# A decoder layer's sparse attention: the compressed keys are set in front of the selected keys, so that one product gives both scores for six of eight query tiles

## The chip, the cores and the metric

The kernel runs on one core of one Trainium2 chip. The metric is device time in microseconds (us) for one execution of the whole program. The profile is of one such execution; its engines are PE (matrix products), DVE (vector), ACT (activation functions), POOL (a second, slower vector engine) and SP (which issues transfers).

## What is computed

One decoder layer on 1024 tokens of width 1024: a sparse attention ("NSA", eight query heads in two key groups) and a latent attention ("MLA", eight heads) side by side, merged by gates, then a gated feed-forward part with a short convolution, then a gated input embedding. The change is in NSA. Each query there attends three times, and the three results are gated and added:

```python
# compressed: 63 keys per group, each made from 32 tokens (stride 16)
s_c = einsum('btgrd,bjgd->bgrtj', q, k_cmp) * scale - slopes * dist_c
p_cmp = masked_softmax(s_c, dist_c >= 0)          # dist_c = t - end of block j
o_cmp = einsum('bgrtj,bjgd->btgrd', p_cmp, v_cmp)
# selected: the 16 best blocks of 64 keys; with 1024 tokens there are 16, so all of them
s = einsum('bcgrd,bgckld->bgrckl', qc, kg) * scale - slopes * dist
pr = masked_softmax(s, dist >= 0)
o_sel = einsum(..., pr, vg)
# window: the last 512 keys
o_win = einsum('bgrqs,bsgd->bqgrd', masked_softmax(...), vblk)
o = g[:, :, 0] * o_cmp + g[:, :, 1] * o_sel + g[:, :, 2] * o_win
```

The softmax of each of the three is its own: own maximum, own sum.

## The kernel before

**Tiles and units.** The 1024 queries are eight tiles of 128, numbered i. NSA goes through them from 7 to 0. For a tile and a key group g (0, 1) there are three units, called by b: b=1 selected, b=2 window, b=0 compressed, in this order. A unit has four heads r of 64 dimensions. A unit's score steps give its probabilities (tokens in partitions, keys along a row); its second part, once per 128 keys, transposes the four heads' block on PE (L885, into a tile `pT`, three buffers), splits it into a rounded high part on ACT (`ph`, L308) and the rest on DVE (`pl`, L309), and multiplies both with the values into `oT` (L894 and L895).

**Keys and queries.** A score is a sum of two 128-row products. `KA` holds the high part of the keys twice, `KB` the low part with two rows for position; `QA` and `QB` are the queries that go with them, `QB` with the slopes. For the compressed keys there are `KAc` and `KBc`, 64 columns wide (63 keys and a zero column). Masks are added by a product of an identity (`identb`, bfloat16) with a table of zeros and -1e30: `mdiag` for the diagonal block, `mfar` for the window's far end, `mcmp` for compressed keys not yet complete.

**Selected and window scores.** For tiles 4 to 7 `s_step` does one head at a time: `KB` product (L941), masks (L944, L945), `KA` product (L948), into a score tile `sc` of two PSUM banks. `sc` has two buffers in all. DVE takes the row's maximum (L869), ACT the exponential straight from PSUM with the sum on the side (L873), DVE the reciprocal (L875), POOL multiplies by sum and gate (L954). Rows of up to 512 keys stand in one bank, longer ones are two halves. For tiles 0 to 3 `s_group` does four heads (tiles 0, 1) or two (tiles 2, 3) in one `sc` tile (L979, L981, L983; maximum L985, exponential L987). A product is never less than 256 columns wide there.

**Compressed scores.** `c_step` is a score step of its own. Per head it has three products of 64 columns (L915, L916, L917). Then, on all four heads in one instruction each: maximum (L920), its clamp (L921) and the subtraction into `PC` in SBUF (L922) on DVE, the exponential on ACT (L924), the sum (L925), its clamp, reciprocal and gate (L926 to L928) on DVE, the product on POOL (L929). `PC` is one buffer for all tiles.

**Order.** `attend` gives every score step and every block step a time in steps of a list and sorts by it; unit k's score steps lie between `lo` and `last`, and each unit's `lo` is no earlier than the `last` of the unit before it. A scheduler that simulates the engines then settles the order of instructions on each engine. PE, DVE and ACT run their instructions in order. The branch products of an earlier part (L303 to L305) are strewn in as fills in the later tiles.

## Time and profile before

| what | us |
|---|---|
| runs | 1784.37, 1789.68, 1800.34; median 1789.68 |
| the profiled execution | 1789.02, its span 1787.2 |
| first NSA product to the end of tile 4's scores | 407 to 580 of the span |
| tiles 3 to 0 of NSA | 580 to about 692 |
| busy over the span: PE, weight load, DVE, ACT, POOL | 1713.3, 1403.3, 1272.1, 860.8, 292.1 |

A busy time says how long an engine had an instruction in it. PE's instructions overlap: the time from the start of one to the start of the next is what one of them takes of PE; its own duration is longer. Where an engine idles, the row says which engine's instruction ended the wait.

### The profile page before, as it was taken

To read this page: it belongs to the slowest core of one execution; us is meant where nothing else is said; L and a number is where in the kernel's file an instruction comes from. 1 tells how busy PE (TensorE), PEld (TensorE's weight loads), DVE (VectorE), ACT (ScalarE), POOL (GpSimd) and SP (SyncE) were. 2 spreads that over 40 slices of the span, in tenths; PEclk is the share of its full clock that TensorE was granted. 3 is DMA by queue.
4 is the path that set the end of the run, shared out by engine and by line. 5 is a ranking of instruction groups with operands and counts; after the bars stand their busy time and mean duration, and the time that the engine had idled before them with its cause. 6 is when DMAs were issued, how large, how long until landed. Compare 5 with 4: busy or idle time off the path is not lost.

```text
span 1787.2 us, 23559 instructions
## 1 busy us (share of the span) xinstructions
PE 1713.3 (96%) x8537; PEld 1403.3 (79%) x8537; DVE 1272.1 (71%) x2030; ACT 860.8 (48%) x1537; POOL 292.1 (16%) x435
## 2 busy tenths in 40 slices
PE   8969899999999999999899999999999998999998
PEld 7857688887777787887678887888888876887886
DVE  6557754425888887787765698888888879767553
ACT  6433332325777766666543354444444443345321
POOL 3000004003555544333401000000000000001010
PEclk8989899999999999999999999999999999999999
DMA  5295242200001225656383112222223292438111
GB/s 194 80 243 154 71 134 69 59 25 30 1 1 37 89 70 158 149 151 183 110 261 109 57 55 83 83 83 94 71 83 94 71 348 87 147 122 274 58 59 47
DMA packets 182512, 191.94 MB, mean 107 GB/s; under 512 B 12805, under 2 KB 136125, under 8 KB 182397
## 3 DMA queue, kind: packets, MB, share of 16 engines
q1 hardware_dynamic: 175292, 180.91, 33.2%
q10 hardware_dynamic: 7104, 9.54, 1.5%
q8 instruction: 67, 1.10, 0.2%
q14 instruction: 49, 0.39, 0.1%
HBM read 142.96 MB, written 47.45 MB: 107 GB/s over the span
## 4 chain that ended last, share of the span: by engine, by line
PE 80%; DVE 8%; DMA 7%; ACT 2%; issue 2%; SPq 1%; POOL 1%; DVEq 0%; POOLq 0%; ACTq 0%
PE big L304 9%; PE big L303 9%; PE big L305 9%; PE pT L303 6%; PE pT L304 6%; PE pT L305 6%; PE pT L885 5%; PE one L303 3%; PE one L304 3%; PE one L305 3%; PE oT L895 3%; PE oT L894 3%; DMA k_d<-kx 1%; DVE wlo L309 1%; PE sc L948 1%
## 5 line engine op out<-in xcount | busy, mean ns | idle before, releaser
L345 POOL TENSOR_SCALAR stat<-stat 128x1 f32<-128x1 f32 (+1 forms) x48 | 18.2, 380 | 892.5 <-ACT yn L1278 624.9
L309 DVE TENSOR_TENSOR pl<-pT,ph 128x512 fp32r<-128x512 f32 (+1 forms) x244 | 149.6, 630 | 13.7 <-ACT ph L308 12.2
L308 ACT ACTIVATE ph<-pT 128x512 fp32r<-128x512 f32 (+1 forms) x244 | 130.1, 555 | 60.7 <-PE pT L885 52.9
L303 PE MATMUL big<-hh,rh 128*128 128x512 f32 x380 | 148.2, 390 | 2.5 <-ACT e L220 1.0
L304 PE MATMUL big<-hl,rh 128*128 128x512 f32 x380 | 148.0, 389 | 0.0
L305 PE MATMUL big<-hh,rl 128*128 128x512 f32 x380 | 147.5, 389 | 0.0
L869 DVE TENSOR_REDUCE mx<-sc 128x1 f32<-128x640 f32 (+7 forms) x128 | 106.6, 835 | 32.4 <-PE sc L948 22.6
L308 ACT ACTIVATE rh<-S 128x512 fp32r<-128x512 f32 x100 | 62.8, 629 | 115.3 <-PE big L304 78.0
L1401 DVE SCALAR_TENSOR_TENSOR u<-C,wcT,u 128x1024 f32<-128x1024 f32 x88 | 111.0, 1280 | 3.7 <-ACT u L1397 3.2
L308 ACT ACTIVATE rh<-wraw 128x512 fp32r<-128x512 f32 x83 | 51.9, 630 | 114.2 <-PE big L304 47.1
L304 PE MATMUL big<-wlo,whi 128*128 128x512 f32 x242 | 97.0, 401 | 9.9 <-DVE wlo L309 9.9
L305 PE MATMUL big<-whi,wlo 128*128 128x512 f32 x242 | 95.2, 393 | 0.0
L303 PE MATMUL pT<-hh,whi 128*128 128x512 f32 x224 | 89.8, 401 | 5.1 <-DVE kx L309 3.3
L303 PE MATMUL big<-whi 128*128 128x512 f32 x242 | 91.3, 393 | 2.4 <-ACT whi L308 2.4
L304 PE MATMUL pT<-hl,whi 128*128 128x512 f32 x224 | 89.0, 397 | 0.0
L305 PE MATMUL pT<-hh,wlo 128*128 128x512 f32 x224 | 88.9, 398 | 0.0
L303 PEld LDWEIGHTS big<-hh,rh 128*128 128x128 f32 x380 | 71.2, 188 | 18.6 <-ACT e L220 1.5
L309 DVE TENSOR_TENSOR rl<-S,rh 128x512 fp32r<-128x512 f32 x100 | 68.7, 689 | 22.0 <-ACT rh L308 21.9
L304 PEld LDWEIGHTS big<-hl,rh 128*128 128x128 f32 x380 | 71.4, 188 | 15.0 <-DVE hl L309 0.4
L305 PEld LDWEIGHTS big<-hh,rl 128*128 128x128 f32 x380 | 71.4, 188 | 14.8
L308 ACT ACTIVATE whi<-wraw 128x1024 fp32r<-128x1024 f32 x40 | 42.1, 1058 | 53.0 <-DVE wraw L1463 20.9
L304 PEld LDWEIGHTS big<-wlo,whi 128*128 128x128 f32 x242 | 45.9, 190 | 24.7 <-DVE wlo L309 15.4
(543 smaller groups left out, 5003.2 us busy)
## 6 DMA issues: line engine op xcount, KB each, us to landing
wraw<-in_w_up_dram SPq DMA_DIRECT2D x44, 512.0 KB, 3.9
wraw<-in_w_in_dram SPq DMA_DIRECT2D x24, 512.0 KB, 4.7
g<-gm_d SPq DMA_DIRECT2D x48, 256.0 KB, 3.4
wraw<-in_w_down_dram SPq DMA_DIRECT2D x47, 256.0 KB, 3.3
g_d<-u SPq DMA_DIRECT2D x22, 512.0 KB, 2.6
wraw<-g_d SPq DMA_DIRECT2D x36, 256.0 KB, 3.0
xt<-in_x_dram SPq DMA_DIRECT2D x16, 512.0 KB, 6.8
gm_d<-gms ACTq DMA_DIRECT2D x16, 512.0 KB, 2.9
```

What stands on the lines that cost most here:

```text
L303: nc.tensor.matmul(ps, lh, rh, start=start, stop=False, skip_group_check=more)
L304: nc.tensor.matmul(ps, lh, rl, start=False, stop=False, skip_group_check=more)
L305: nc.tensor.matmul(ps, ll, rh, start=False, stop=stop, skip_group_check=more)
L308: nc.scalar.activation(hi, ps, AF.Copy)
L309: nc.vector.tensor_sub(lo, ps, f32(hi))
L345: nc.gpsimd.tensor_scalar(st, st, EPS, None, op0=OP.add)
L869: nc.vector.tensor_reduce(u.nm[:, r:r + 1], src, axis=AX.XY, op=OP.max, negate=True)
L885: nc.tensor.transpose(pT[:m, r], cols(r), ident)
L894: nc.tensor.matmul(oT[:, a:], v, ph, start=first, stop=False)
L895: nc.tensor.matmul(oT[:, a:], v, pl, start=False, stop=last)
L948: nc.tensor.matmul(ps[:, si, :w], q_part(0, 128, i, 4 * g + r), KA[b - 1][g][:, k0 + o:k0 + o + w], start=False, stop=True)
L1401: nc.vector.scalar_tensor_tensor(u[s], C[s][:, 2 - sh:2 - sh + T], wcT[:, 2 - sh, ch:ch + 1], u[s], op0=OP.mult, op1=OP.add)
```

## The change

The compressed keys and the selected keys of a group now stand in one tile, `CKA` and `CKB`, 64 + 1024 columns: `KAc`, `KBc` are its first 64 columns, `KA[0]`, `KB[0]` the rest. For the selected unit of tiles 0, 1, 2, 4, 5, 6 the first 64 columns are scored in the same product as the selected keys (`c0` = 64), the mask `mcmp` is added there, and `c_heads` does the compressed softmax from the score tile: maximum (L924 of the new file) per head or group on DVE, one exponential of 64 columns per head straight from PSUM with its sum (L929), reciprocal and gate (L934, L935), POOL's product into a new tile `pcm` of two buffers. Tiles 3 and 7, whose rows of 512 and 1024 keys leave no room in the banks, keep `c_step`. The selected unit of tile 1 is done in two groups of two heads. The compressed unit has no score step for the six tiles, and a unit without score steps no longer moves `last`.

```diff
--- before.py
+++ after.py
@@ -256,7 +256,8 @@
         lo = max(lo, last, start[k] - 24.0)
         if u.after is not None:
             lo = max(lo, start[k - 1] + u.after)
-        last = max(start[k] - 8.0, lo + 1.0)
+        if u.S:
+            last = max(start[k] - 8.0, lo + 1.0)
         if u.hook is not None:
             ev.append((start[k] + u.at, -1, u.hook))
         for j, f in enumerate(u.S):
@@ -704,10 +705,10 @@
     Vc = [vp0([128, 128], F32R, f"Vc{g}") for g in range(2)]
     V0 = vp0([128, 4, 4, 128], F32R, "V0")
     kv = Pool("kv", side="left")
-    KA = [[kv([128, T], F32R, f"KA{b}{g}") for g in range(2)] for b in range(2)]
-    KB = [[kv([128, T], F32R, f"KB{b}{g}") for g in range(2)] for b in range(2)]
-    KAc = [kv([128, 64], F32R, f"KAc{g}") for g in range(2)]
-    KBc = [kv([128, 64], F32R, f"KBc{g}") for g in range(2)]
+
+    CK = [[kv([128, 64 + T], F32R, f"C{n}{g}") for g in range(2)] for n in ("KA", "KB")]
+    KA, KB = ([[c[:, 64:] for c in CK[n]], [kv([128, T], F32R, f"K{'AB'[n]}1{g}") for g in range(2)]] for n in range(2))
+    KAc, KBc = ([c[:, :64] for c in CK[n]] for n in range(2))
 
     sm = Pool("sm", side="right")
     gls = [sm([64, 126], F32, f"gl{n}") for n in range(2)]
@@ -909,6 +910,31 @@
         segs = segments(n)
         pc = PC
 
+        both = b < 2 and i not in (3, 7)
+        c0 = 64 if both and b else 0
+
+        def c_heads(r0, n_r, src):
+
+            if r0 == 0:
+                c = st["pc", i, g] = Unit()
+                stats_of(c)
+                c.P = bq([128, 4, 64], F32, "pcm", bufs=2)
+            c = st["pc", i, g]
+            nm = c.nm[:, r0:r0 + n_r]
+            nc.vector.tensor_reduce(nm, src, axis=AX.X, op=OP.max, negate=True)
+            if i == 0:
+                nc.vector.tensor_scalar(nm, nm, 1e20, None, op0=OP.min)
+            for j in range(n_r):
+                r = r0 + j
+                nc.scalar.activation(c.P[:, r], src[:, j], AF.Exp, bias=c.nm[:, r:r + 1], accum_out=c.sums[:, r:r + 1])
+            if r0 + n_r == 4:
+                sums = c.sums
+                if i == 0:
+                    nc.vector.tensor_scalar(sums, sums, 1e-30, None, op0=OP.max)
+                nc.vector.reciprocal(sums, sums)
+                nc.vector.tensor_mul(sums, sums, gates[:, i, g * 4:g * 4 + 4])
+                nc.gpsimd.tensor_tensor(c.P, c.P, sums[:, :, None].to_broadcast([128, 4, 64]), op=OP.mult)
+
         def c_step():
             ps = two_banks()[:, 0, :256].rearrange("p (b m) -> p b m", m=64)
             for r in range(4):
@@ -937,17 +963,27 @@
                     u.P = [P[:, j] for j in range(4)]
                     stats_of(u)
                 ps = two_banks()
+
+                def keys(si, o, w, K):
+                    if c0 and si == 0:
+                        return ps[:, 0, :64 + w], K[0][g][:, :64 + w]
+                    return ps[:, si, c0:c0 + w], K[1][b - 1][g][:, k0 + o:k0 + o + w]
+
                 for si, (o, w) in enumerate(segs):
-                    nc.tensor.matmul(ps[:, si, :w], qb[:, r], KB[b - 1][g][:, k0 + o:k0 + o + w],
-                                     start=True, stop=False)
+                    out_, k_ = keys(si, o, w, (CK[1], KB))
+                    nc.tensor.matmul(out_, qb[:, r], k_, start=True, stop=False)
+                if c0:
+                    nc.tensor.matmul(ps[:, 0, :64], identb, mcmp[:, i], start=False, stop=False)
                 if b == 2:
                     nc.tensor.matmul(ps[:, 0, :128], identb, mfar, start=False, stop=False)
-                nc.tensor.matmul(ps[:, len(segs) - 1, segs[-1][1] - 128:segs[-1][1]], identb, mdiag,
-                                 start=False, stop=False)
+                e = c0 + segs[-1][1]
+                nc.tensor.matmul(ps[:, len(segs) - 1, e - 128:e], identb, mdiag, start=False, stop=False)
                 for si, (o, w) in enumerate(segs):
-                    nc.tensor.matmul(ps[:, si, :w], q_part(0, 128, i, 4 * g + r), KA[b - 1][g][:, k0 + o:k0 + o + w],
-                                     start=False, stop=True)
-                src = row_max(u, r, ps, n)
+                    out_, k_ = keys(si, o, w, (CK[0], KA))
+                    nc.tensor.matmul(out_, q_part(0, 128, i, 4 * g + r), k_, start=False, stop=True)
+                if c0:
+                    c_heads(r, 1, ps[:, 0:1, :64])
+                src = row_max(u, r, ps[:, :, c0:], n)
                 pv = u.P[r][:, :n]
                 row_exp(u, r, pv, src)
                 c = b * 8 + g * 4 + r
@@ -972,19 +1008,24 @@
                         u.P[r] = PL["pS"]([128, 512], F32, "pS", bufs=6)
                 w = 1024 // n_r
                 ps = two_banks().rearrange("p a (b m) -> p (a b) m", m=w)
-                w = max(n, 256)
+                w = max(c0 + n, 256)
+                ka, kb = ((CK[a][g] if c0 else K[b - 1][g])[:, :w] for a, K in enumerate((KA, KB)))
                 for j in range(n_r // 2):
                     pair = (j, j + n_r // 2)
                     for r in pair:
-                        nc.tensor.matmul(ps[:, r, :w], qb[:, r0 + r], KB[b - 1][g][:, :w], start=True, stop=False)
+                        nc.tensor.matmul(ps[:, r, :w], qb[:, r0 + r], kb, start=True, stop=False)
                     for r in pair:
-                        nc.tensor.matmul(ps[:, r, n - 128:n], identb, mdiag, start=False, stop=False)
+                        if c0:
+                            nc.tensor.matmul(ps[:, r, :64], identb, mcmp[:, i], start=False, stop=False)
+                        nc.tensor.matmul(ps[:, r, c0 + n - 128:c0 + n], identb, mdiag, start=False, stop=False)
                     for r in pair:
-                        nc.tensor.matmul(ps[:, r, :w], q_part(0, 128, i, 4 * g + r0 + r), KA[b - 1][g][:, :w],
-                                         start=False, stop=True)
-                nc.vector.tensor_reduce(u.nm[:, r0:r0 + n_r], ps[:, :, :n], axis=AX.X, op=OP.max, negate=True)
+                        nc.tensor.matmul(ps[:, r, :w], q_part(0, 128, i, 4 * g + r0 + r), ka, start=False, stop=True)
+                if c0:
+                    c_heads(r0, n_r, ps[:, :, :64])
+                keys = ps[:, :, c0:c0 + n]
+                nc.vector.tensor_reduce(u.nm[:, r0:r0 + n_r], keys, axis=AX.X, op=OP.max, negate=True)
                 for r in rs:
-                    nc.scalar.activation(u.P[r][:, :n], ps[:, r - r0, :n], AF.Exp, bias=u.nm[:, r:r + 1],
+                    nc.scalar.activation(u.P[r][:, :n], keys[:, r - r0], AF.Exp, bias=u.nm[:, r:r + 1],
                                          accum_out=u.sums[:, r:r + 1])
                 nc.vector.reciprocal(u.sums[:, r0:r0 + n_r], u.sums[:, r0:r0 + n_r])
                 c = b * 8 + g * 4
@@ -995,17 +1036,18 @@
             return run
 
         if b == 0:
-            u.S = [c_step]
+            u.S = [] if both else [c_step]
         elif i >= 4:
             u.S = [s_step(r) for r in range(4)]
         else:
-            n_r = 2 if i > 1 else 4
+            n_r = 2 if i > 1 or i == 1 and b == 1 else 4
             u.S = [s_group(r, n_r) for r in range(0, 4, n_r)]
         if b == 1:
             u.S.insert(0, lambda: q_form(i, g))
 
         def t_front(j):
-            return lambda: front(u, j, lambda r: u.P[r][:, j * 128:(j + 1) * 128] if b else u.P[r], 0, 128 if b else 64)
+            return lambda: front(u, j, lambda r: u.P[r][:, j * 128:(j + 1) * 128] if b else
+                                 st["pc", i, g].P[:, r] if both else u.P[r], 0, 128 if b else 64)
 
         def t_back(j):
             def run():
```

The first place is PE between the scores of tile 6 group 0 and group 1. Before (`QB_3215` is group 0's query tile, `QB_3216` group 1's; `hh` and `hl` are buffers of probabilities):

```order
L894 MATMUL oT<-ph,V_2317 128x512
L885 MATMUL pT<-ident,hh_3846 128x128 x4
L915 MATMUL sc<-KBc_2331,QB_3215 128x64
L916 LDWEIGHTS identb
L916 MATMUL sc<-mcmp,identb 128x64
L917 MATMUL sc<-KAc_2329,QA_2712 128x64
...
L885 MATMUL pT<-ident,hh_3846 128x128 x4
L941 MATMUL sc<-KB_2326,QB_3216 128x448 x2
L945 LDWEIGHTS identb
L945 MATMUL sc<-mdiag,identb 128x128
L948 MATMUL sc<-KA_2322,QA_2712 128x448 x2
```

After, the same place (lines of the new file; L886 is the transposition, L895 and L896 the products with the values):

```order
L895 MATMUL oT<-ph,V_2317 128x512
L886 MATMUL pT<-ident,hh_3842 128x128 x4
L974 MATMUL sc<-CKB_2324,QB_3212 128x512
L974 MATMUL sc<-CKB_2324,QB_3212 128x448
L976 LDWEIGHTS identb
L976 MATMUL sc<-mcmp,identb 128x64
L980 LDWEIGHTS identb
L980 MATMUL sc<-mdiag,identb 128x128
L983 MATMUL sc<-CKA_2322,QA_2708 128x512
L983 MATMUL sc<-CKA_2322,QA_2708 128x448
```

The twelve products of `c_step` (four of the three shown) are gone from between the two units; each selected head has its first half 64 columns wider and one mask product more.

The second place is ACT in the same stretch, from the last window heads of group 0 to the second selected head of group 1. Before:

```order
L873 ACTIVATE hl_3977,sums<-sc,mx 128x640 x2
L308 ACTIVATE ph<-pT 128x512 x2
L924 ACTIVATE PC<-PC 128x256
L308 ACTIVATE ph<-pT 128x512 x2
L873 ACTIVATE hl_4112,sums<-sc,mx 128x896
L308 ACTIVATE ph<-pT 128x512
L873 ACTIVATE hl_4112,sums<-sc,mx 128x896
```

After:

```order
L874 ACTIVATE hl_3991,sums<-sc,mx 128x640 x2
L309 ACTIVATE ph<-pT 128x512
L929 ACTIVATE pcm,sums<-sc,mx 128x64
L309 ACTIVATE ph<-pT 128x512
L874 ACTIVATE hl_4069,sums<-sc,mx 128x896
L309 ACTIVATE ph<-pT 128x512
L929 ACTIVATE pcm,sums<-sc,mx 128x64
L309 ACTIVATE ph<-pT 128x512 x2
L874 ACTIVATE hl_4069,sums<-sc,mx 128x896
```

One exponential of 256 columns a unit has become one of 64 columns ahead of each head's own, with copies `ph` queued behind it.

The third place is DVE in that stretch. Before:

```order
L920 TENSOR_REDUCE mx<-sc 128x4
L309 TENSOR_TENSOR pl<-pT,ph 128x512
L921 TENSOR_SCALAR mx<-mx 128x4
L922 TENSOR_TENSOR PC<-sc,mx 128x256
L309 TENSOR_TENSOR pl<-pT,ph 128x512
L869 TENSOR_REDUCE mx<-sc 128x1
L925 TENSOR_REDUCE sums<-PC 128x4
L309 TENSOR_TENSOR pl<-pT,ph 128x512
L926 TENSOR_SCALAR sums<-sums 128x4
```

After:

```order
L924 TENSOR_REDUCE mx<-sc 128x1
L310 TENSOR_TENSOR pl<-pT,ph 128x512
L870 TENSOR_REDUCE mx<-sc 128x1
L310 TENSOR_TENSOR pl<-pT,ph 128x512
L924 TENSOR_REDUCE mx<-sc 128x1
L876 RECIPROCAL sums<-sums 128x1
L310 TENSOR_TENSOR pl<-pT,ph 128x512
L870 TENSOR_REDUCE mx<-sc 128x1
```

Of `c_step`'s seven instructions the clamps, the subtraction and the sum are gone; its maximum is now one small instruction ahead of each head's own.

## Rows read from the trace of the kernel before

**Rows 1.** The windows view of two stretches of the span: NSA tiles 7 to 4, and NSA tiles 3 to 0. Columns: stretch, its length, busy us (and instructions) of PE, of its weight load, of DVE, ACT and POOL, granted clock of PE as a share, busy share of the DMA engines, GB/s.

```profile
407.00:580.00 173.00, 169.49 (x1082) 135.86 (x1080) 137.49 (x286) 120.70 (x248) 81.35 (x92) 1.00 0.06 16
580.00:692.00 112.00, 110.92 (x702) 88.53 (x701) 91.55 (x195) 78.30 (x218) 58.90 (x90) 1.00 0.30 85
```

**Rows 2.** The waits view of PE in 407 to 692, all its rows: the waiting instruction, whom it waited for, us in total, times, the longest.

```profile
PE oT L894 <- DVE osum L1032: 1.3, 2, 0.7
PE oT L895 <- DVE pl L309: 1.2, 5, 0.3
PE sc L941 <- ACT hl L873: 0.6, 3, 0.3
PE sc L915 <- ACT hl L873: 0.5, 1, 0.5
PE sc L979 <- ACT pS L987: 0.4, 1, 0.4
PE oT L894 <- ACT ph L308: 0.3, 1, 0.3
PE sc L979 <- ACT hl L987: 0.2, 1, 0.2
```

**Rows 3.** The timeline of PE over tile 7 group 1's compressed scores: start, duration, line, tiles, shape, count. The rows left out are the second and third head and most of the fourth, which read alike; the last row is the next instruction.

```profile
478.33 0.30 PE L915 MATMUL sc<-KBc,QB 128*128 128x64 f32 x1
478.47 0.20 PE L916 MATMUL sc<-mcmp,identb 128*128 128x64 bf16 x1
478.51 0.28 PE L917 MATMUL sc<-KAc,QA 128*128 128x64 f32 x1
...
479.32 0.28 PE L917 MATMUL sc<-KAc,QA 128*128 128x64 f32 x1
479.44 0.47 PE L895 MATMUL oT<-pl,V 128*128 128x512 f32 x1
```

**Rows 4.** The timeline of PE at places where products of other widths follow each other: a window head's masks, and MLA's scores of 320 and 512 columns.

```profile
474.79 0.23 PE L944 MATMUL sc<-mfar,identb 128*128 128x128 bf16 x1
474.86 0.22 PE L945 MATMUL sc<-mdiag,identb 128*128 128x128 bf16 x1
...
704.07 0.40 PE L1090 MATMUL sc<-hh 96*128 96x512 f32 x1
704.31 0.39 PE L1091 MATMUL sc<-hh 96*128 96x512 f32 x1
...
708.60 0.31 PE L1091 MATMUL sc<-hl 96*128 96x320 f32 x1
708.75 0.31 PE L1095 MATMUL sc<-hl 96*128 96x320 f32 x1
```

**Rows 5.** The view of instruction groups by shape, DVE, 407 to 880: line, tiles, shapes, count, busy us in all, mean ns of one, idle before.

```profile
L985 DVE TENSOR_REDUCE mx<-sc 128x4 f32<-128x1024 f32 x4 | 4.9, 1222 | 1.2 <-PE sc L983 1.2
L985 DVE TENSOR_REDUCE mx<-sc 128x4 f32<-128x512 f32 x4 | 2.8, 688 | 0.8 <-PE sc L983 0.7
L920 DVE TENSOR_REDUCE mx<-sc 128x4 f32<-128x256 f32 x16 | 6.7, 421 | 3.6 <-PE sc L917 3.2
L922 DVE TENSOR_TENSOR PC<-sc,mx 128x256 f32<-128x256 f32 x16 | 6.7, 421 | 1.4 <-PE pT L885 0.3
L925 DVE TENSOR_REDUCE sums<-PC 128x4 f32<-128x256 f32 x16 | 6.5, 408 | 0.2
L921 DVE TENSOR_SCALAR mx<-mx 128x4 f32<-128x4 f32 x16 | 4.3, 267 | 0.2
L926 DVE TENSOR_SCALAR sums<-sums 128x4 f32<-128x4 f32 x16 | 2.8, 174 | 0.0
L927 DVE RECIPROCAL sums<-sums 128x4 f32<-128x4 f32 x16 | 2.7, 169 | 0.1
L928 DVE TENSOR_TENSOR sums<-sums,gates 128x4 f32<-128x4 f32 x16 | 2.6, 161 | 0.2
L869 DVE TENSOR_REDUCE mx<-sc 128x1 f32<-128x128 f32 x8 | 2.3, 286 | 1.4 <-PE sc L1095 1.3
```

**Rows 6.** The same view, ACT: `c_step`'s exponential, the two narrowest exponentials from PSUM, and the instruction that fetches a sum.

```profile
L924 ACT ACTIVATE PC<-PC 128x256 f32<-128x256 f32 x16 | 6.6, 414 | 1.3 <-DVE PC L922 0.5
L987 ACT ACTIVATE pS<-sc,mx 128x256 f32<-128x256 f32 x8 | 3.7, 476 | 0.0
L987 ACT ACTIVATE pS<-sc,mx 128x128 f32<-128x128 f32 x8 | 2.9, 367 | 0.2 <-PE pT L885 0.2
L987 ACT ACTIVATION_READ_ACCUMULATOR pS<-sc,mx 128x1 f32 x32 | 6.7, 209 | 0.0
```

**Rows 7.** The timeline of ACT where two exponentials with sums follow each other in tile 3, with only the fetch of the first one's sum between them.

```profile
601.08 0.69 ACT L987 ACTIVATE pS<-sc,mx 128x512 f32<-128x512 f32 x1
...
601.74 0.70 ACT L987 ACTIVATE pS<-sc,mx 128x512 f32<-128x512 f32 x1
```

**Rows 8.** The waits view of ACT in 407 to 692, its largest row.

```profile
ACT ph L308 <- PE pT L885: 38.8, 52, 2.0
```

**Rows 9.** The timeline of PE and of ACT at the first and the third selected head of tile 6 group 0: the starts of their first products, and the first head's exponential.

```profile
480.34 0.65 PE L941 MATMUL sc<-KB,QB 128*128 128x448 f32 x2
...
483.68 1.00 ACT L873 ACTIVATE hl<-sc,mx 128x896 f32<-128x896 f32 x1
...
485.83 0.65 PE L941 MATMUL sc<-KB,QB 128*128 128x448 f32 x2
```

## The prediction, made blind

> **What bounds the kernel now.** I read the windows of the NSA stage first, then what PE waited for there, then single starts on PE. In the two stretches PE is busy 169.5 of 173 and 110.9 of 112 us, DVE 137.5 and 91.6 (79% and 82%), ACT 120.7 and 78.3 (70% both), at the full granted clock (2.4 GHz) [rows 1]. Busy alone doesn't make PE the bound, since one of its products lies over the next. But the waits of PE in these 285 us come to 1.3 + 1.2 + 0.6 + 0.5 + 0.4 + 0.3 + 0.2 = 4.5 us [rows 2], and starts follow each other as closely as the columns let them: 0.24 us for a 512-column product, 0.15 for a 320-column one [rows 4]. The largest wait of ACT is for transpositions from PE, 38.8 us [rows 8]: ACT is held up by PE and not the other way. So in this stage the price of a product is the time to the next start, and work taken from PE should come off the end nearly whole; work on DVE and ACT has cover as long as PE's few waits don't grow. After the stage comes MLA, which begins on PE where NSA ends, so what is won here is moved forward and not lost in a gap.
>
> **PE, removed.** Four heads of compressed scores take from 478.33 to 479.44, 1.11 us [rows 3]. By head that is 0.14 for the KB product, 0.04 for the mask, and some 0.1 for the KA product: a product of 64 columns costs most of what 256 would. Of 16 units 12 lose this: 12 x 1.11 = 13.3 us.
>
> **PE, added.** Going from 320 to 512 columns lengthens a start by 0.24 - 0.15 = 0.09 [rows 4], so 64 more columns cost 0.03; two products a head, 40 heads of tiles 1, 2, 4, 5, 6: 2.4 us. Tile 0 pays none, since its 128 + 64 columns still fit the 256 that were run anyway. The mask is now one more product in each of 48 heads: 0.04 beside its neighbours in c_step [rows 3], 0.07 for the 128 columns of the far mask [rows 4]. I take 0.04, the same instruction: 1.9 us (3.4 at the other end). The mask stands where another mask product already stood, so no further change between number formats comes with it. Added 4.3. **Net on PE: 13.3 - 4.3 = 9.0 us less.**
>
> **DVE.** c_step's seven instructions are 0.421 + 0.267 + 0.421 + 0.408 + 0.174 + 0.169 + 0.161 = 2.02 us a unit [rows 5]. A maximum over 64 columns has no row; 128 columns are 0.286, 256 are 0.421, so by the same slope 64 are 0.22, and no less than the 0.16 of an instruction on four numbers. Tiles 4 to 6 (six units) now pay 4 x 0.22 + 0.169 + 0.161 = 1.21. Tiles 1 and 2 (four units) pay two maxima over 2 x 64, 2 x 0.286 + 0.33 = 0.90. Tile 0 (two units) keeps its clamps: 0.42 + 0.27 + 0.17 + 0.33 = 1.19. Tile 1's split makes two maxima of 0.69 from one of 1.22, with one reciprocal more (0.17): 0.3 for each of two units, 0.6. Saved: 6 x 0.81 + 4 x 1.12 + 2 x 0.83 - 0.6 = 10.4 us. DVE isn't the bound, so I enter none of it; it pays for the next part.
>
> **ACT.** c_step's one exponential was 0.41. In its place stand four of 64 columns with sums. No row has that width; 0.476 at 256 and 0.367 at 128 give 0.11 per 128 columns, so some 0.31 at 64, and one with its fetch of the sum takes about its own duration to the next start (0.66 for one of 0.69) [rows 6, 7]. So 4 x 0.31 = 1.24, and 0.83 more a unit: 12 x 0.83 = 10 us on ACT in all. If the fetch (0.21) came on top each time it would be 10 + 48 x 0.21 = 20 us. ACT has 86 us of the 285 free [rows 1], and 38.8 of them stand ahead of the copies `ph`, waiting for PE. Entered at nothing: PE's lead over ACT hides it. If that cover fails, the copies `ph` that queue behind each small exponential come late, and PE's products with the values after them.
>
> **POOL, transfers, order.** POOL's product over 4 x 64 columns is the same as before. No transfer is added; two branch loads change places with their neighbours in SP's queue. Each selected head holds its score buffer longer by the small maximum, 0.22, since the head's own maximum queues behind it on DVE; the small exponential runs on ACT while that maximum runs. On the other side twelve score tiles fewer are taken from the same two buffers. At tile 6 the first head's products start at 480.34, its exponential ends at 483.68 + 1.00, and the head that takes the same buffer starts at 485.83 [rows 9]: 1.15 us are free, five times what the small maximum adds. Nothing entered.
>
> **Sum.** The profiled execution took 1789.0 (span 1787.2), 0.7 under the median of the runs. 1789.0 - 9.0 = 1780.0. By the ends of the terms above (mask 0.07, or all of PE's 4.5 us of waits falling away with DVE's saved work) this runs from 1775.5 to 1781.5; with 10 us of ACT half uncovered, to 1785.
>
> A rule speaks against it. PE's weight load is busy 135.9 of 173 us, 79%, while PE's products show 98% [rows 1]. The Trainium skill (Trainium Kernel Development and Optimization, Performance Expectations) holds that the busy time of matrix products is a bad measure of how near a kernel is to its limit, because they are pipelined, and that the share of weight loading is a better one. By that a fifth of PE is slack, and taking work from it need give nothing; the sum would be 0 in place of -9.0. The waits and the starts don't bear it out, so it is a rival with a small chance.
>
> **Rivals.**
> 1. PE isn't the bound (the rule above): the round from transposition over `ph` and `pl` to the products sets the pace, PE's freed time turns into waits, and the time stays at 1789, between 1786 and 1792. For it: PE's busy time overstates; ACT and DVE are both over 70%. Against: 4.5 us of waits in 285. Chance 0.06.
> 2. ACT's queue eats the gain: 48 small exponentials stand ahead of copies `ph`, and their 10 us reach PE in full (half: 1785): 1780 + 10 = 1790. For it: ACT is in order, and PE already waits at times for exponentials (0.6 + 0.5 + 0.4 + 0.2) [rows 2]. Against: ACT's 38.8 us of waiting for PE [rows 8]. Chance 0.12.
> 3. The freed DVE time helps as well: PE's waits for `pl`, `osum` and for buffers shrink, and unit after unit runs with one change of product kind less. The waits are worth 4.5 and all of DVE's 10.4 would be the far end: 1780 - 4.5 to 1780 - 10.4, so 1770 to 1775. For it: the longest waits are for DVE [rows 2]. Against: they are short. Chance 0.11.
> 4. Slower: the score buffers. If each of the 48 heads is released later by small maximum, small exponential and fetch, 0.22 + 0.31 + 0.21 = 0.74, and PE stands for all of it, that is 48 x 0.74 = 35.5, less the 9.0 won: 1815. It decides from the point where a buffer is held longer than PE takes to come round to it again; at tile 6 the room is 1.15 us, so it needs heads that stand closer than those, as in tile 1's two groups and wherever window heads follow. Chance 0.05.
>
> **How the numbers follow.** The likeliest, 1775.5 to 1785, has 0.66. The range takes rival 1, rival 2 and most of the third with it: 1771 to 1792, which leaves out rival 4 and the tails. One per cent of the median is 17.9 us, about what a measurement of this kernel can tell from no change (the three runs lie 16 us apart). Faster by that means below 1771.8: the far end of rival 3, and scatter, 0.09. Slower means above 1807.6: rival 4, 0.05. Between: 0.86. The predicted time is 1780.
>
> **What would show it.** Right: the compressed products fall from 64 to 16 of each kind; NSA's stretch, 285 us before, is shorter by 8 to 10 and what follows has its old length; the 64-column exponentials last 0.3 us; DVE works about 10 us less and ACT about 10 more; PE's waits stay near 4.5 us. Wrong: PE's waits for `ph` or for score buffers rise by several us (rivals 2, 4), or its starts draw apart with no wait named (rival 1). The sum would fail most easily at the 1.11 us, if its neighbours already filled part of it, or at ACT's cover in tiles 2 to 0, where groups of heads send several exponentials at once.

## The result, and the profile after

The changed kernel is 0.6% slower: 1800.99 us in the median against 1789.43 of the kernel before, ratio 1.0061, 95% interval 1.0047 to 1.0075. That is 11 us the wrong way, where 9 the right way were forecast; the time lies outside the range given, 1771 to 1792. "Between" the one-per-cent bounds, given 0.86, came true, but by luck: it was meant for a gain of 9 us, and none came. The profiled execution took 1803.94 us (before 1789.02). Its page, busy time of each engine:

```profile
span 1800.8 us, 23446 instructions
PE 1714.7 (95%) x8441; PEld 1396.5 (78%) x8441; DVE 1265.0 (70%) x2012; ACT 872.5 (48%) x1621; POOL 294.4 (16%) x435
```

DVE does 7.1 us less than before and ACT 11.7 more, nearly what was said. PE has 96 instructions fewer, yet is busy no shorter. The waits view of PE in NSA, and then over the 16 us in which NSA gives way to MLA (line, tile, whom it waited for, us in total, times, the longest):

```profile
PE sc L974 <- ACT hl L874: 3.5, 9, 0.7
PE oT L896 <- DVE pl L310: 1.4, 4, 0.6
PE sc L974 <- ACT hh L874: 1.1, 1, 1.1
PE oT L895 <- DVE osum L1074: 1.0, 3, 0.7
...
PE sc L1132 <- ACT pS L1028: 3.2, 2, 2.7
```

Before, all waits together were 4.5 us and those for score buffers the smaller part [rows 2]. Now the largest are PE's waits to write scores (`sc`) until an exponential (L874, L1028) has read the buffer. Behind the 2.7 us one something else shows. The windows view of that place (length, then busy us of PE, weight load, DVE, ACT, POOL, and the granted clock):

```profile
680.00:684.00 4.00, 4.00 (x34) 3.43 (x32) 2.75 (x6) 2.53 (x11) 2.61 (x5) 1.00 0.44 133
684.00:688.00 4.00, 1.86 (x10) 0.96 (x9) 3.69 (x10) 3.34 (x12) 0.61 (x1) 1.00 0.46 132
688.00:692.00 4.00, 3.47 (x12) 2.04 (x13) 0.89 (x3) 1.65 (x10) 2.43 (x5) 0.71 1.04 222
692.00:696.00 4.00, 3.47 (x14) 2.59 (x13) 2.40 (x7) 2.94 (x11) 2.24 (x6) 0.50 0.18 45
696.00:700.00 4.00, 4.00 (x11) 3.09 (x11) 0.59 (x3) 0.67 (x2) 1.60 (x3) 0.51 0.00 0
700.00:704.00 4.00, 4.00 (x27) 3.26 (x26) 3.13 (x6) 2.28 (x4) 0.00 (x0) 1.00 0.42 118
```

PE stands, and from about 690 to 700 its clock is granted at half (1.2 GHz). The kernel before has 16.00 us of PE work at a clock of 1.00 between 684 and 700. The timeline of PE there, 512-column products:

```profile
697.05 0.63 PE L304 MATMUL pT<-hh,dh 128*128 128x512 f32 x1
697.48 0.63 PE L305 MATMUL pT<-hh,dh 128*128 128x512 f32 x1
```

They start 0.43 us apart in place of 0.24 [rows 4].

To set traces side by side I use three moments that every kernel has: DVE's first addition of `osum` for tile 7 group 0, for tile 4 group 1, and for tile 0 group 1. These are the rows, before and after:

```profile
453.19 0.84 DVE L1032 TENSOR_TENSOR osum<-oT,otmp 64x256 f32<-64x256 f32 x2
597.20 0.84 DVE L1032 TENSOR_TENSOR osum<-oT,otmp 64x256 f32<-64x256 f32 x2
701.13 0.85 DVE L1032 TENSOR_TENSOR osum<-oT,otmp 64x256 f32<-64x256 f32 x2 [0.16 <-ACT otmp L1028]
```

```profile
452.18 0.84 DVE L1074 TENSOR_TENSOR osum<-oT,otmp 64x256 f32<-64x256 f32 x2
597.59 0.84 DVE L1074 TENSOR_TENSOR osum<-oT,otmp 64x256 f32<-64x256 f32 x2
707.69 0.84 DVE L1074 TENSOR_TENSOR osum<-oT,otmp 64x256 f32<-64x256 f32 x2
```

So tiles 6 to 4 (with the rest of tile 7 group 1, whose work is unchanged) take 145.4 us in place of 144.0, tiles 3 to 0 take 110.1 in place of 103.9, and MLA to the first product of the stage after it 180.7 in place of 178.1 (the rows of that third moment are not shown). In all +10.1. The same three stretches, and how long a selected head's scores are held, for every kernel run below. "Hold" is the mean over the 16 selected heads of tiles 6 and 5, from the end of the head's last score product to the end of its own exponential, read from the timelines of PE and ACT.

| kernel | tiles 6-4 | tiles 3-0 | MLA | hold | time against before |
|---|---|---|---|---|---|
| before | 144.0 | 103.9 | 178.1 | 2.63 | |
| after | 145.4 | 110.1 | 180.7 | 4.08 | 1.0061 |
| tile0_as_before | 145.4 | 104.8 | 180.0 | | 1.0024 |
| tiles_4_to_6_only | 145.4 | 103.8 | 181.2 | | 0.9996 |
| tile_0_only | 144.0 | 105.2 | 178.0 | | 0.9992 |
| own_first | 143.3 | 101.5 | 181.0 | 2.38 | 0.9993 |
| no_small_softmax | 136.3 | 99.1 | 177.0 | 2.34 | 0.9921 |
| clock_kept_up | 145.4 | 106.2 | 178.0 | 4.07 | 1.0035 |
| small_exp_twice | 152.9 | 109.0 | 180.4 | 5.00 | 1.0081 |
| copy_out | 140.6 | 104.3 | 179.7 | 2.75 | 0.9979 |
| copy_then_own_first | 140.7 | 101.6 | 181.4 | 2.75 | 0.9989 |
| no_small_max | 139.2 | 107.2 | 180.5 | 3.17 | 0.9967 |
| own_max_first | 139.3 | 105.7 | 179.5 | 2.98 | 0.9998 |
| max_first_then_own_first | 139.3 | 101.5 | 181.7 | 2.98 | 0.9981 |

The three stretches are of one execution each. Where kernels have the same code in tiles 6 to 4 they agree within 0.1 us (145.4 four times, 144.0 twice). MLA has the same code in all fourteen and doesn't agree: it takes 177.0 to 178.1 in four traces, 179.7 to 181.7 in the nine whose granted clock falls in MLA's last 35 us, and 179.5 in `own_max_first`, where it doesn't fall there. So that column shows first of all where the clock fell in the execution profiled, not what an edit did in MLA.

### The profile page after: what moved, and what is told of

Same layout as the page of the kernel before. It is cut to its first block, busy times and chain, and to the rows that moved or that the text cites. A ratio compares the mean times of both kernels' runs of the same rounds, so it can differ in the third digit from the quotient of the medians.

```text
span 1800.8 us, 23446 instructions
## 1 busy us (share of the span) xinstructions
PE 1714.7 (95%) x8441; PEld 1396.5 (78%) x8441; DVE 1265.0 (70%) x2012; ACT 872.5 (48%) x1621; POOL 294.4 (16%) x435
## 4 chain that ended last, share of the span: by engine, by line
PE 78%; DVE 8%; DMA 7%; ACT 4%; issue 2%; SPq 1%; POOL 0%; DVEq 0%; POOLq 0%; ACTq 0%
PE big L305 9%; PE big L304 9%; PE big L306 9%; PE pT L304 6%; PE pT L305 6%; PE pT L306 6%; PE pT L886 4%; PE one L304 3%; PE one L305 3%; PE one L306 3%; PE oT L896 3%; PE oT L895 3%; DMA k_d<-kx 1%; PE sc L974 1%; PE sc L983 1%
```

## Where the hold comes from

The prediction gave a head's score buffer 0.22 us more; it is 4.08 - 2.63 = 1.45. One head shows why: tile 6 group 1, the third selected head. The timelines of PE, DVE and ACT (start, duration; the bracket is idle time and who ended it), before:

```profile
486.36 0.65 PE L948 MATMUL sc<-KA,QA 128*128 128x448 f32 x2
...
487.05 1.09 DVE L869 TENSOR_REDUCE mx<-sc 128x1 f32<-128x896 f32 x1 [0.46 <-PE sc L948]
...
488.28 1.00 ACT L873 ACTIVATE hl<-sc,mx 128x896 f32<-128x896 f32 x1
```

The scores are done at 487.01, DVE stands ready for them, and the exponential ends at 489.28, 2.27 us later. After the change:

```profile
485.48 0.68 PE L983 MATMUL sc<-CKA,QA 128*128 128x512 f32 x2
...
487.05 0.21 DVE L924 TENSOR_REDUCE mx<-sc 128x1 f32<-128x64 f32 x1
487.18 0.15 DVE L876 RECIPROCAL sums<-sums 128x1 f32<-128x1 f32 x1
488.03 0.69 DVE L310 TENSOR_TENSOR pl<-pT,ph 128x512 fp32r<-128x512 f32 x1 [0.70 <-ACT ph L309]
488.64 1.08 DVE L870 TENSOR_REDUCE mx<-sc 128x1 f32<-128x896 f32 x1
...
487.40 0.60 ACT L309 ACTIVATE ph<-pT 128x512 fp32r<-128x512 f32 x1 [0.33 <-PE pT L886]
487.89 0.31 ACT L929 ACTIVATE pcm<-sc,mx 128x64 f32<-128x64 f32 x1
489.75 1.01 ACT L874 ACTIVATE hl<-sc,mx 128x896 f32<-128x896 f32 x1 [0.86 <-DVE mx L870]
```

The scores are done at 486.16. The small maximum runs at 487.05, but the head's own maximum, on scores that lie ready, starts only at 488.64. Between the two in DVE's queue stand a reciprocal and a copy `pl`, and the `pl` waits 0.70 us for ACT's `ph`, which waits for a transposition on PE. ACT then waits 0.86 for the own maximum. The exponential ends at 490.76: 4.6 us. So the small maximum doesn't cost its 0.2 us; it splits the head's maxima, and DVE's other work, with its own waits, comes in between. Over the 16 heads the own maximum starts 1.43 us behind the small one in the mean, about the whole 1.45.

PE meets this at the window heads that follow in the same two buffers. All 4.4 us that it waits for score buffers in tiles 6 to 4 stand ahead of a window head's first product; the longest two, at tile 6 group 0:

```profile
474.33 0.56 PE L974 MATMUL sc<-KB,QB 128*128 128x320 f32 x2 [1.11 <-ACT hh L874]
...
477.20 0.56 PE L974 MATMUL sc<-KB,QB 128*128 128x320 f32 x2 [0.72 <-ACT hl L874]
```

## The experiments

Two theories were written down first. **B**, buffers: the small maxima and exponentials hold the two score buffers in every tile. **H**, hand-over: the loss arises where NSA ends in tile 0. The edits are against the changed kernel. The expectations say TensorE for PE, VectorE for DVE, ScalarE for ACT and GpSimd for POOL.

**tile0_as_before**

```
-        both = b < 2 and i not in (3, 7)
+        both = b < 2 and i not in (0, 3, 7)
```

> The changed kernel, but tile 0 keeps its compressed score step of its own (five tiles are joined, not six). Theory H (handoff): the loss sits where NSA gives way to MLA. At tile 0 DVE's clamp of the compressed sums stands in its queue ahead of two maxima and waits 1.5 us for ACT's small exponentials, PE then waits 2.7 us for a score buffer and runs at the lower clock for some 10 us. By H this kernel has no such wait at the handoff, the clock stays up there, and it comes back by 7 to 10 us: 1791 to 1794, and a little under the 1789 of before if the other five tiles keep their gain. Theory B (buffers): score buffers held longer by the small maximum and the small exponentials cost PE in every tile, the handoff is one such place among many. By B it comes back by 2 to 4 us only: 1797 to 1799.

1794.19 us, ratio 1.0024 (1.0007 to 1.0040). The 3.2 us row for L1132 is gone and the clock is 1.00 from 684 to 700. That takes 0.0037 of the ratio away, 6.6 us; none of the forecast's 9 appears. The time lies at the upper end of H's range and below B's.

**tiles_4_to_6_only**

```
-        both = b < 2 and i not in (3, 7)
+        both = b < 2 and i in (4, 5, 6)
...
-            n_r = 2 if i > 1 or i == 1 and b == 1 else 4
+            n_r = 2 if i > 1 else 4
```

> Only tiles 4, 5 and 6 have the compressed keys in front; tiles 0 to 3 and 7 are as before. By the sum of the prediction six units save 0.83 us of PE each, 5 us: 1784.5. Theory H: that gain comes, 1784 to 1786, since nothing is changed at the handoff. Theory B: the window heads that follow wait for score buffers, the gain of the stretch is the 1 us that the trace of the changed kernel shows there: 1788 to 1790.

1789.29, ratio 0.9996 (0.9977 to 1.0014): three tiles with half of all the small softmax work gain nothing, far from any hand-over: their stretch takes 145.4 us, 1.4 more than before. That speaks for B.

**tile_0_only**

```
-        both = b < 2 and i not in (3, 7)
+        both = b < 2 and i == 0
...
-            n_r = 2 if i > 1 or i == 1 and b == 1 else 4
+            n_r = 2 if i > 1 else 4
```

> Only tile 0 has the compressed keys in front. Theory H: the wait of 2 to 3 us at the handoff and the low clock behind it come with this tile alone: 1795 to 1799 beside 1789 of before. Theory B: two units of sixteen, 1788 to 1791.

1789.06, ratio 0.9992 (0.9978 to 1.0006), in B's range. H as stated falls: tile 0 alone isn't enough for the loss. PE's wait at that place is 1.3 us here, not 2.7, and the clock falls for a shorter time (0.57 in one stretch of 4 us).

**own_first**

```
-                if c0:
-                    c_heads(r, 1, ps[:, 0:1, :64])
                 src = row_max(u, r, ps[:, :, c0:], n)
                 pv = u.P[r][:, :n]
                 row_exp(u, r, pv, src)
+                if c0:
+                    c_heads(r, 1, ps[:, 0:1, :64])
```

and the same in `s_group`.

> All six tiles joined, but in program order a head's own maximum and exponential come first and the compressed softmax after them. Theory H: at tile 0 the two maxima no longer stand behind the clamp of the compressed sums, PE's wait at the handoff shrinks below 1 us: 1786 to 1793. Theory B: the buffers are held as long in sum, since the compressed exponentials are now last in the buffer: 1799 to 1803.

1789.21, ratio 0.9993 (0.9968 to 1.0018): the same work in another order takes the whole loss away. That lies in H's range and far from B's, and 8.6 of the 10.7 us that it gains on the changed kernel in NSA lie in tiles 3 to 0, where the clock stays at 1.00; PE's wait at the hand-over is 1.3, though, and not below 1. In tiles 6 to 4 the head's own exponential ends 2.38 us after its scores. But the buffer isn't free then: the small exponential, now last, ends 3.6 us after them, so these tiles gain only 0.7 on the kernel before. Neither theory alone has the loss: H's hand-over and B's buffers are both in it.

**no_small_softmax**

```
-            nm = c.nm[:, r0:r0 + n_r]
-            nc.vector.tensor_reduce(nm, src, axis=AX.X, op=OP.max, negate=True)
...
-                nc.scalar.activation(c.P[:, r], src[:, j], AF.Exp, ...)
...
+                nc.gpsimd.memset(c.P, 0.0)
```

> Leaves out the softmax of the compressed scores in the six tiles: no maximum, exponential, reciprocal or gate product, the matrix of weights is set to zero on GpSimd instead; the wide products, the masks and all that TensorE does with the weights stay, so TensorE has exactly the changed kernel's work. Theory B (the small maxima and exponentials, run ahead of the head's own, hold the score buffers and use up TensorE's 9 us): 1778 to 1784, NSA stretch to the end of tile 0 shorter than before's 247.9 by 6 to 10. Rival P (the 9 us were never there: the wide products and the masks cost TensorE more than their prices in the trace of before): 1786 to 1792, that stretch within 2 us of 247.9.

1774.7, ratio 0.9921 (0.9893 to 0.9948). PE has exactly the changed kernel's products and the time falls by 13.4 us, more than the 9.0 of the sum. Part of this isn't PE's price: PE's waits are fewer than before (3.1 us in 406 to 684, for 4.5), and DVE and ACT are rid of compressed work that the kernel before did too (busy 1256.0 and 855.7). The largest wait is

```profile
PE oT L895 <- ACT pS L1016: 1.1, 2, 0.8
```

Rival P is out by its own figures: the stretch is 12.5 us shorter, not within 2. How much of the 9 comes off with all the softmax work in place, `own_max_first` and `max_first_then_own_first` show below.

**clock_kept_up**

```
         pT = bank().rearrange("p (a b) -> p a b", b=128)
         for r in range(a, 4):
             nc.tensor.transpose(pT[:m, r], cols(r), ident)
+        if u is st.get("last"):
+            dm = bank()
+            for _ in range(10):
+                nc.tensor.matmul(dm, identb, mcmp.rearrange("p a b -> p (a b)"), start=True, stop=True)
...
+    st["last"] = second[-4]
```

> The changed kernel with ten more products of 512 columns (identity by compressed masks, result unused) in TensorE's queue right behind the last compressed weights' transposes, where TensorE stands 2.7 us for the exponentials ahead of MLA's first score. They take the wait's place, not more. If the fall to half clock behind that wait is what costs (theory H, second half): the granted clock stays at 1.00 between 680 and 700 us, first MLA scores .23 apart for 512 columns, 1795 to 1798 us. If the wait alone costs and the clock's fall is made good elsewhere: 1800 to 1803.

1793.65, ratio 1.0035 (1.0019 to 1.0051), by the ratios 4.6 us less than the changed kernel. Up to the last tile the trace repeats that of the changed kernel within 0.1 us (all of it lies 5.4 us earlier here); then the clock stays up:

```profile
680.00:684.00 4.00, 3.50 (x19) 1.96 (x19) 3.21 (x10) 3.95 (x16) 1.24 (x3) 1.00 0.79 197
684.00:688.00 4.00, 3.01 (x18) 1.82 (x16) 1.57 (x6) 2.51 (x10) 2.35 (x6) 1.00 0.84 199
688.00:692.00 4.00, 4.00 (x22) 3.11 (x21) 2.18 (x7) 1.95 (x6) 3.25 (x7) 1.00 0.02 4
692.00:696.00 4.00, 4.00 (x27) 3.19 (x27) 3.29 (x7) 2.38 (x5) 0.00 (x0) 1.00 0.72 199
```

Products that compute nothing make the kernel faster: tiles 3 to 0 are 3.9 us shorter and MLA 2.7 than in the changed kernel. PE begins MLA's scores no earlier (236.3 us after the first moment in both), so these 6.6 us go with the clock and not with the wait. But not all of them are of the hand-over: followed through MLA, the lead is 4.7 us until MLA's last 35 us and grows by 1.9 only there, where the clock of the changed kernel falls a second time and here stays at 1.00:

```profile
864.00:868.00 4.00, 2.52 (x9) 1.46 (x9) 4.00 (x8) 3.44 (x10) 1.20 (x2) 0.89 0.79 242
868.00:872.00 4.00, 4.00 (x15) 3.36 (x14) 3.12 (x9) 1.61 (x5) 2.10 (x2) 0.68 0.46 145
```

Kernels whose clock stays up at the hand-over fall at MLA's end too (`tile0_as_before`, `own_first`), so it isn't shown that the second fall follows from the first. The fall at the hand-over cost 4.7 us in these traces.

**small_exp_twice**

```
+                nc.scalar.activation(c.P[:, r], src[:, j], AF.Exp, bias=c.nm[:, r:r + 1], accum_out=c.sums[:, r:r + 1])
```

(a second time, right behind the first).

> The changed kernel with each of the 48 small exponentials issued twice (the second overwrites the first with the same values): ScalarE gets 48 times 0.42 = 20 us more, TensorE and VectorE nothing. Theory B: ScalarE's work ahead of the head's own exponential goes into the score buffers' hold and so into the end, mostly one for one: 1811 to 1821. Rival Q (ScalarE's queue is covered, and the loss comes from VectorE's order or from the hand-over to MLA alone): 1800 to 1805.

1804.8, ratio 1.0081 (1.0053 to 1.0109): at the upper end of rival Q's range. The page has ACT busy 885.2 us, 12.7 more than in the changed kernel and not 20 (start to start a small exponential with its fetch takes 0.3). They cost some 4 us of the time, which the two kernels' intervals can't tell from none, but 7.5 in tiles 6 to 4, where traces repeat within 0.1. "Mostly one for one" falls on the time, and "covered" on that stretch: ACT's exponentials count, but they aren't most of it.

**copy_out**

```
...
+            nc.vector.tensor_copy(c.P[:, r0:r0 + n_r], src)
+
+        def c_soft():
...
```

with `c_step`'s softmax on that copy as the step of unit b=0, and the copy right behind the head's own maximum.

> The wide products stay, but the compressed scores are copied out of PSUM by VectorE (one copy a head, behind the head's own maximum), and their softmax is the one of the kernel before, for four heads at once from SBUF, in a step of its own where the compressed step stood: one exponential of 256 columns on ScalarE instead of four with sums read back. TensorE has the changed kernel's work, ScalarE that of before, VectorE some 8 us more than before. Theory B: score buffers are held only by a copy (0.2 us), so most of the 9 us comes out: 1780 to 1786. Rival P: 1788 to 1793.

1784.44, ratio 0.9979 (0.9961 to 0.9997), in B's range: hold 2.75, tiles 6 to 4 shorter by 3.4 than before, although DVE does 7.5 us more than before (page: 1279.6). By the ratio it is 3.8 us faster than before, so not "most of the 9".

**no_small_max** and **own_max_first** part DVE's order from ACT's load. The first:

```
-            nc.vector.tensor_reduce(nm, src, axis=AX.X, op=OP.max, negate=True)
...
-                nc.scalar.activation(c.P[:, r], src[:, j], AF.Exp, bias=c.nm[:, r:r + 1], accum_out=c.sums[:, r:r + 1])
+                nc.scalar.activation(c.P[:, r], src[:, j], AF.Exp, scale=1e-3, accum_out=c.sums[:, r:r + 1])
```

> The changed kernel without the small maxima on VectorE: the compressed scores' exponentials take no shift (and the scores times 0.001, so that nothing overflows), all else stays, the 48 exponentials with their sums on ScalarE too. It leaves out the shift of the compressed softmax. Of the changed kernel's distance to no_small_softmax (about 26 us), if the small exponentials in ScalarE's queue ahead of the head's own carry most: 1794 to 1801. If the chain through VectorE's maximum, for which ScalarE stands still before each small exponential, carries most: 1778 to 1787.

1785.55, ratio 0.9967 (0.9946 to 0.9988): with all 48 exponentials in place, taking the maxima away gives some 16 us against the changed kernel. The second leaves no work out:

```
-                if c0:
-                    c_heads(r, 1, ps[:, 0:1, :64])
                 src = row_max(u, r, ps[:, :, c0:], n)
+                if c0:
+                    c_heads(r, 1, ps[:, 0:1, :64])
```

and the same in `s_group`.

> All the work of the changed kernel; only the head's own maximum goes ahead of the small maximum on VectorE, while ScalarE still makes the small exponential ahead of the head's own (in own_first both were behind). It parts VectorE's order from ScalarE's. In tile 6 and 5 the changed kernel holds a selected head's scores 4.1 us from the last score product to the end of the head's own exponential (before: 2.6), since VectorE makes the small maximum, then a copy pl, and only then the head's own maximum. If that order carries the loss (theory B, VectorE's half): the hold falls to 2.6 to 3.2, tiles 6 to 4 take 139 to 143 us in place of 145.4, and the time is 1784 to 1791. If the 48 small exponentials in ScalarE's queue carry it: the hold stays over 3.5, and the time is 1794 to 1801.

1789.17, ratio 0.9998 (0.9985 to 1.0011); by the ratio 11 us less than the changed kernel; hold 2.98, tiles 6 to 4 139.3, time, hold and stretch all as DVE's half of B said. The same third head in its timelines:

```profile
482.22 0.68 PE L983 MATMUL sc<-CKA,QA 128*128 128x512 f32 x2
...
482.94 1.09 DVE L870 TENSOR_REDUCE mx<-sc 128x1 f32<-128x896 f32 x1 [0.38 <-PE sc L983]
483.95 0.22 DVE L924 TENSOR_REDUCE mx<-sc 128x1 f32<-128x64 f32 x1
...
484.56 0.31 ACT L929 ACTIVATE pcm<-sc,mx 128x64 f32<-128x64 f32 x1
484.85 1.01 ACT L874 ACTIVATE hl<-sc,mx 128x896 f32<-128x896 f32 x1
```

The own maximum starts 0.04 us after the scores, the small one lies right behind it, and ACT makes both exponentials by 485.86: 2.96 us in place of 4.6. Of the 4.7 us that tiles 6 to 4 gain against before, tiles 3 to 0 give back 1.8 and MLA 1.4. At the hand-over the clock falls again, to 0.50 until 688, and PE's waits just ahead have only 0.4 and 0.5 us:

```profile
676.00:680.00 4.00, 3.22 (x9) 1.73 (x8) 3.14 (x8) 3.45 (x11) 2.40 (x6) 0.75 0.94 198
680.00:684.00 4.00, 4.00 (x12) 2.31 (x12) 1.29 (x4) 0.57 (x2) 2.09 (x5) 0.50 0.50 122
```

**copy_then_own_first**: `copy_out` in tiles 6 to 4, `own_first` below.

```
...
+            if i >= 4:
+                nc.vector.tensor_copy(c.P[:, r0:r0 + n_r], src)
+                return
...
```

> Tiles 4 to 6 as in copy_out (the compressed scores copied out by VectorE behind the head's own maximum, softmax for four heads at once), tiles 2 to 0 as in own_first (the small softmax behind the head's own exponentials). In copy_out tiles 6 to 4 took 140.6 us where before took 144.0, in own_first the tiles below and the start of MLA 101.5 where before took 103.9. If each is the work of its own stretch, as theory B has it: the sum 242.1 against 247.9, so 1781 to 1785 us, ratio 0.996 to 0.998. If what one stretch gains is given back in the next (the hand-over to MLA waits for ScalarE or a DMA): 1786 to 1790.

1786.34, ratio 0.9989 (0.9973 to 1.0005): the stretches add up as said (242.3 for 242.1), but the time lies in the range of "given back" and can't be told from before. In the trace MLA takes 3.3 us more than before; the clock is at 1.00 at the hand-over and falls in MLA's last 35 us.

**max_first_then_own_first**: `own_max_first` in `s_step` (tiles 6 to 4), `own_first` in `s_group` (tiles 2 to 0).

> All the work of the changed kernel, in another order: in tiles 6 to 4 the head's own maximum first, then the small maximum, the small exponential and the head's own (own_max_first, 139.3 us there against 144.0 before); in tiles 2 to 0 the head's own maximum and exponentials first, the small softmax behind them (own_first, 101.5 us with the start of MLA against 103.9). If each gain belongs to its own stretch: 240.8 us from the end of tile 7's first half to the end of NSA against 247.9, so 7 us less, 1781 to 1785, with the clock at 1.00 where NSA gives way to MLA. If the clock falls there as in own_max_first: 1785 to 1789.

1784.61, ratio 0.9981 (0.9966 to 0.9995): some 15 us better than the changed kernel, and 3.4 better than the one before by the ratio, with the same instructions in another order. NSA's two stretches sum to 240.8, as said, 7.1 less than before, and the clock stays at 1.00 where NSA gives way to MLA. MLA gives back 3.6 of it in the profiled execution, at its end, where the clock falls again behind a stretch in which PE is half idle:

```profile
848.00:852.00 4.00, 1.94 (x10) 0.87 (x8) 3.97 (x6) 2.75 (x7) 1.27 (x1) 0.98 0.44 131
852.00:856.00 4.00, 3.57 (x10) 2.76 (x11) 4.00 (x10) 3.67 (x10) 0.66 (x2) 0.50 0.44 138
856.00:860.00 4.00, 4.00 (x16) 3.25 (x15) 1.60 (x5) 0.64 (x1) 1.92 (x2) 0.66 0.62 191
```

## Why the prediction was wrong, step by step

- **PE's prices were right.** By their starts, the compressed products of the first stretch fell from 7.4 to 1.8 us and the wider scores rose from 46.6 to 48.6. That this comes off the end is shown with all the work in place: in `own_max_first` tiles 6 to 4 are 4.7 us shorter than before, where the prediction's prices give 6 x 1.11 - 24 x 0.10 = 4.3, and in `max_first_then_own_first` NSA is 7.1 shorter of the 9.0. Rival 1 is out. The Trainium skill (Trainium Kernel Development and Optimization, Performance Expectations) calls the busy time of matrix products a bad measure, because they are pipelined, and the share of weight loading one of the good ones. The slack of a fifth that rival 1 read from that share, these runs don't bear out.
- **The instructions' prices on DVE and ACT were right.** In groups by shape:

```profile
L924 DVE TENSOR_REDUCE mx<-sc 128x1 f32<-128x64 f32 x24 | 5.2, 217 | 1.1 <-PE sc L983 0.8
L929 ACT ACTIVATE pcm<-sc,mx 128x64 f32<-128x64 f32 x48 | 14.9, 315 | 4.4 <-DVE mx L924 3.1 <-DVE mx L926 1.1
```

  0.22 and 0.31 had been said. ACT's load (11.7 for 10) came near; DVE's saving was a third short (7.1 for 10.4).
- **The failing step is "each selected head holds its score buffer longer by the small maximum, 0.22".** It priced the added instruction and not the place in the queue that it opens: 1.45. The order of DVE shown with the change, ahead of the prediction, already had a `pl` between the small and the own maximum; the sentence "the head's own maximum queues behind it" left it out. The 1.15 us of room were read at the first of four heads of tile 6 group 1 ([rows 9] calls it group 0; in the same way the scores of [rows 3] are tile 6 group 0's, not tile 7 group 1's). At that head the hold didn't grow (2.90 for 3.17); at the other three it grew by 1.8 to 2.3, more than the room. Rival 4 had the mechanism and, with "wherever window heads follow", the place. Its size was wrong twice: 0.74 a head by the small instructions' own times, and PE standing for all of it.
- **ACT's cover** (rival 2) is a part: in `small_exp_twice` 12.7 us more on ACT cost some 4 of the time, so as an estimate from that run the load here is worth 3 or 4. It isn't the main term.
- **"What is won here is moved forward and not lost in a gap" failed.** The compressed products of tile 0 (684.89 to 685.99 in the trace before) were also what PE did while the last exponentials ran. Without them, and with DVE held up once more (1.52 us idle for the small exponentials' sums), PE stood 2.7 us, and the granted clock fell behind it. It took both: in `tile_0_only`, where the tiles ahead are as before, the wait is 1.3. DVE at that place:

```profile
684.26 0.17 DVE L933 TENSOR_SCALAR sums<-sums 128x4 f32<-128x4 f32 x1 [1.52 <-ACT pcm L929]
684.34 1.28 DVE L1026 TENSOR_REDUCE mx<-sc 128x4 f32<-128x512 f32 x2
```

- **The balance.** The trace of `no_small_softmax` stands 13.7 us ahead of before at MLA's end, that of the changed kernel 10.1 behind. Of these 23.8 us, 6.6 go with the clock (`clock_kept_up`: 4.7 at the hand-over, 1.9 in MLA's last 35 us) and 17.2 with the small softmax, its work, place and order, of which `own_max_first` gives back 6.1 in tiles 6 to 4 alone. So the buffers took the gain away, and the clock has a large part in the step from no gain to a loss. The other runs say the same: the mean granted clock is 0.981 over the 20 runs of the changed kernel and 0.986 over the runs of the kernel before beside the experiments and over those of `clock_kept_up`. 0.005 of 1799 us would be 9 us; as an estimate this is an upper one, since PE isn't always what is waited for.

**Open.** In tiles 6 to 4 the changed kernel takes 9.1 us more than `no_small_softmax`. PE's waits with a named cause are 5.9 us in the one and 1.2 in the other. These rows count from the end of a product, whose duration covers part of a wait. By starts, the time from the product before it to a window head's first score product comes to 8.3 us in the one and 2.4 in the other (27 places each), so 5.8 of the 9.1 lie there. The other 3.3 lie in products whose starts stand further apart with no wait named, and no run says by what. Each edit also lets the scheduler settle the order anew, so a run changes more than its lines.

## What to carry to other kernels

When an instruction is put ahead of another in an in-order queue, price the time from the one to the other in the new order, with what stands between them and what that waits for, not the instruction. With two buffers between a producer and its readers, count until the last reader is done, and start the longest chain of readers first. Work that is taken from the busiest engine may have been its bridge over a wait at the end of a stage: look what it does there once the work is gone.

## What the runs showed of the hardware

The granted clock at the hand-over was not expected to matter: half for some 10 us after PE had stood 2.7 us (row 684 to 688: 1.86 of 4 us busy), 4.7 us of time, and filled with idle products it stayed at full. How long PE stood doesn't alone decide it: in `own_max_first` the clock fell behind waits of 0.4 and 0.5 us, while in `max_first_then_own_first` it stayed at 1.00 over a wait of 1.3 at the same place:

```profile
676.00:680.00 4.00, 2.63 (x15) 1.63 (x15) 3.76 (x11) 3.36 (x15) 1.74 (x4) 1.00 0.55 148
```

What else does was not settled.
